# A streaming encoder layer on one core: the chain that prepares x for the second half begins at the eighth group and takes two steps per group from the sixteenth

## The chip, the core and the metric

The kernel runs on one core of a Trainium2 chip. A core has five engines that run side by side, each with its own instruction queue, which it takes in order: PE (matrix products), DVE (vector operations), ACT (copies, casts and activations), POOL (here mostly issues of DMA stores) and SP (issues of DMA loads). Data lies in DRAM, in the on-chip memory, and in eight PSUM banks into which PE writes. Sixteen DMA engines move data, whoever issues the transfer. The metric is the time of one execution on the device in microseconds (us). Lower is better.

## The reference, cut to what matters

One layer, for 2048 prompt tokens and 32 sample tokens, of width 1024, all in float32:

```
h   = RMSNorm(x)
z   = h @ W_in      # columns: q k v | attention gate | B C conv-in conv-gate | merge gates A, B
A   : sliding-window attention with sinks;        yA = (attn * silu(gA)) @ W_A
B   : v = causal conv of width 3 over (C * u);    yB = (B * v * silu(gB)) @ W_B
r   = x + (sigmoid(mA) * yA + sigmoid(mB) * yB) @ W_o
out = r + sigmoid(r @ W_pg) * (p @ W_pp)
```

The change touches only the first two lines: the normed x (h), and the product with W_in.

## The kernel before

**The product h @ W_in.** Tokens come in two halves, the first of 2 x 512 tokens, the second of 2 x 528 with the sample tokens. Columns of W_in come in 21 groups, each a pair of column blocks: groups 0 to 2 "z" (q, k, v), 3 and 4 "ga" (attention gate), 5, 7, 9, 11 "Cu" (C and conv-in), 6, 8, 10, 12 "Bg" (B and conv gate), 13 to 20 "m" (merge gates). For each half and group, a 2 x 2 block product is formed in seven products p = 1 to 7 rather than eight. For this each group needs four sums of its weight quads (`make_sums`, L352 to L368: four loads a, four sums on DVE at L362 to L365, four stores of the sums by POOL at L368), and each half needs sums and differences of blocks of h.

**One product** (`products`, L649 to L654) is four k by three matmuls: a float32 operand is split in two parts, hi by a cast on ACT (L231) and lo = value - hi on DVE (L232), and high x high, high x low and low x high are added in one bank. Weights w are split this way just before use, from a loaded quad (wr) or a sum (a, sc). A step of the list `steps` is a product (half, group, p). In the first half the order within a group is 7, 5, then 6 of the next group, 3, 4, then 1 and 2 of a group two ahead. When product 5 ends, ACT copies the bank a to a tile u (L843, tile u4 of the group) and DVE subtracts the other bank from u later (L848). Product 3 of the same group writes bank a again, so its first matmul waits for that copy. Results go to `consume`: Cu groups are multiplied and run through the three conv taps on DVE (L704 to L726), Bg groups gate them (L735 to L749), m groups end in an activation and a store.

**The chain X1.** The x of the second half is prepared while the first half is multiplied. `second_half` (L582) is a generator of 14 pieces that `next(X1)` runs one at a time: pieces 1 and 2 the norm factors of the first 528 tokens (ten loads of x on SP at L547, ten squares on ACT at L548, a power on POOL at L525; then a diagonal dg on DVE at L530, five transposes a 128 tokens on PE at L532, copies to rb on ACT at L533 and L535), 3 and 4 the same for the other 528, pieces 5 to 8 the row steps k = 0 to 3 (four loads of xT at L594, four norms on DVE at L555, a combine of four operations on DVE at L559 to L562, seven stores xc by POOL at L599), pieces 9 to 14 the quadrants (two loads of xc at L622, a combine of four half-width operations at L559 to L562, four stores xt at L626). After step (0, 20, 2) the kernel takes whatever is left of the chain and reads xc and xt back.

**What sets the order.** `prep` (L1267) is a list of step numbers. After each of these steps one piece of X1 is issued. The tile framework's scheduler then orders every engine's instructions by its own estimate of times, so that the place in `prep` sets roughly where a piece lies, and the neighbours on each engine follow from the scheduler. Loads get their buffers from shared pools (weight quads, and tiles of x and b), so that a load on SP's queue can wait until an earlier tile has been read or stored.

Of the kernel before, what the change touches and what calls it, by code (L numbers as in the profile page):

```python
# [42 lines left out]
def tile_hybrid_stream_step(ctx: ExitStack, tc: tile.TileContext, x, xT, pT, wu, consts, rope, ckT, cv_dup,  # L43
# [201 lines left out]
    G = len(groups)  # L245
# [26 lines left out]
    for gs in sets:  # L272
        g, e = gs[0], gs[-1]
# [624 lines left out]
    def conv_split(b, cs=range(4)):  # L898
        nt = blk(b)[1]
        for c in cs:  # L900
            yc[b, c] = pair(f"ycs{b}_{c}")
            split_half(yc[b, c][0][:, :nt], yc[b, c][1][:, :nt], conv_in.pop((b, c))[:, :nt])
# [342 lines left out]
    at_step = {x: i for i, todo in enumerate(steps) for x in todo}  # L1245
# [18 lines left out]
    conv_at = {(1, G - 2, 1): lambda: conv_load(0), (1, G - 2, 6): lambda: (conv_split(0), conv_load(1)),  # L1264
               (1, G - 1, 6): lambda: conv_split(1), (1, G - 2, 5): lambda: conv_load(2)}
    conv_at.update({(1, sets[-1], 3 + c % 2, "DE"[c // 2]): lambda c=c: conv_split(2, (c,)) for c in range(4)})
    prep = [at_step[0, g, 7] for g in range(5, G)]  # L1267
    for i, todo in enumerate(steps):
        if i < NS:
            continue  # L1270
# [956 lines left out]
```

## Time and profile before

| | |
|---|---|
| median of 3 runs | 1521.99 us (1521.4 to 1523.32) |
| the profiled execution | 1519.46 us |
| its span | 1517.6 us |
| HBM traffic in the span | 246.53 MB read, 130.04 MB written, 248 GB/s |
| PE's clock | 0.998 of full speed, mean |

The span is the time from the first to the last record on the engines. The rows of the profile name an engine, a line, the tile written and the tiles read, a shape and a count. The chain of work that ended last is to 71% PE. The first half of the product with W_in, with the chain X1 beside it, ends near 470 us, and X1 fills roughly 150 to 420 us of it. The same profile by fortieths of the span (37.9 us each), in tenths of busy time:

```profile
PE   9999999989999999999999999999999999999998
DVE  7896778775568887798976978878899999676777
```

### The profile page before, as it was taken

Reading aid. Unit: us, or ns where it says so; the run is one execution under the profiler, and the core shown is the slowest. Engines: PE = TensorE matmul, PEld = TensorE weight load, DVE = VectorE, ACT = ScalarE, POOL = GpSimd, SP = SyncE. Lnnn points to the kernel's source line nnn. Section 1 sums busy time; section 2 is a strip of 40 time slices with the busy share of each in tenths; the row PEclk is TensorE's granted clock in tenths of the full one; section 3 lists DMA queues with packets and bytes.
Section 4 is the critical chain, followed back from the end, with each engine's and each line's share of the span. In section 5 each row is a group of like instructions: output and inputs, shape, how many; then the busy total and the mean of one; then the engine's idle time right before and its main releaser. Section 6 shows DMA issues by size and latency. Waiting matters only on the chain.

```text
span 1517.6 us, 28008 instructions
## 1 busy us (share of the span) xinstructions
PE 1494.1 (98%) x9553; PEld 1350.3 (89%) x9553; DVE 1211.4 (80%) x2310; ACT 801.1 (53%) x1908; POOL 399.0 (26%) x582
## 2 busy tenths in 40 slices
PE   9999999989999999999999999999999999999998
PEld 7878777778889999999999999998888888999998
DVE  7896778775568887798976978878899999676777
ACT  8453442334457655443456645687765686442453
POOL 2133233232201253344333321113232202211201
PEclk9999999999999999999999999999999999999999
DMA  9479987787777897643477975678888958989959
GB/s 357 152 273 346 323 301 276 266 280 246 242 235 241 301 318 246 218 144 123 135 252 263 334 244 185 215 246 242 273 214 271 243 172 246 308 253 273 263 168 286
DMA packets 206670, 378.34 MB, mean 249 GB/s; under 512 B 24896, under 2 KB 58496, under 8 KB 206528
## 3 DMA queue, kind: packets, MB, share of 16 engines
q1 hardware_dynamic: 160608, 258.30, 52.3%
q0 software_dynamic: 36272, 100.44, 22.2%
q10 hardware_dynamic: 9648, 17.83, 3.2%
q8 instruction: 75, 1.23, 0.3%
q14 instruction: 67, 0.55, 0.1%
HBM read 246.53 MB, written 130.04 MB: 248 GB/s over the span
## 4 chain that ended last, share of the span: by engine, by line
PE 71%; DVE 3%; DMA 3%; issue 1%; ACT 1%; POOL 0%; SPq 0%; ACTq 0%; DVEq 0%; POOLq 0%
PE b L160 21%; PE yB L160 6%; PE yA L160 6%; PE a L649 5%; PE a L654 5%; PE a L651 5%; PE la L787 4%; PE O L160 2%; PE c L654 2%; PE c L651 2%; PE c L649 2%; PE lc L787 2%; PE S L160 2%; PE pp L160 2%; PE PT L160 1%
## 5 line engine op out<-in xcount | busy, mean ns | idle before, releaser
L160 PE MATMUL b<-xb_h,w 128*128 128x264 f32 (+1 forms) x1344 | 310.8, 323 | 1.3 <-DVE at L160 1.3
L160 PEld LDWEIGHTS b<-xb_h,w 128*128 128x128 f32 x1344 | 222.6, 188 | 19.5 <-DVE at L160 1.8
L649 PE MATMUL a<-x_h,w 128*128 128x264 f32 (+1 forms) x744 | 229.4, 322 | 7.3 <-ACT u L843 6.9
L651 PE MATMUL a<-x_l,w 128*128 128x264 f32 (+1 forms) x744 | 229.6, 322 | 0.0
L160 PE MATMUL b<-xb_l,w 128*128 128x264 f32 (+1 forms) x672 | 216.5, 322 | 0.0
L654 PE MATMUL a<-x_h,w 128*128 128x264 f32 (+1 forms) x744 | 200.5, 322 | 1.8 <-DVE w L232 1.8
L231 ACT CAST w<-wr 128x512 fp32r<-128x512 f32 (+1 forms) x180 | 110.3, 619 | 97.7 <-PE c L654 39.3
L649 PEld LDWEIGHTS a<-x_h,w 128*128 128x128 f32 x744 | 140.6, 189 | 19.7 <-ACT u L843 7.8
L232 DVE TENSOR_TENSOR w<-wr,w 128x512 fp32r<-128x512 f32 (+1 forms) x180 | 132.9, 747 | 29.3 <-ACT w L231 29.1
L651 PEld LDWEIGHTS a<-x_l,w 128*128 128x128 f32 x744 | 140.6, 189 | 10.6
L654 PEld LDWEIGHTS a<-x_h,w 128*128 128x128 f32 x744 | 124.8, 189 | 13.9 <-DVE w L232 3.0
L160 PEld LDWEIGHTS b<-xb_l,w 128*128 128x128 f32 x672 | 126.4, 188 | 8.6
L160 ACT CAST w<-wr 128x512 fp32r<-128x512 f32 x120 | 73.8, 623 | 97.4 <-PE b L160 50.9
L787 PE MATMUL la<-x_h,w 128*128 128x264 f32 x516 | 111.5, 285 | 2.5 <-DVE s2n L803 1.2
L649 PE MATMUL c<-x_h,w 128*128 128x512 f32 (+1 forms) x336 | 110.9, 340 | 0.7 <-ACT x_h L160 0.7
L651 PE MATMUL c<-x_l,w 128*128 128x512 f32 (+1 forms) x336 | 110.8, 339 | 0.0
L654 PE MATMUL c<-x_h,w 128*128 128x512 f32 (+1 forms) x336 | 100.6, 340 | 0.0
L231 ACT CAST w<-a 128x512 fp32r<-128x512 f32 x82 | 49.6, 620 | 93.7 <-DVE a L364 43.6
L160 DVE TENSOR_TENSOR w<-wr,w 128x512 fp32r<-128x512 f32 x120 | 83.8, 704 | 18.8 <-ACT w L160 18.4
L848 DVE SCALAR_TENSOR_TENSOR u<-u,c 128x264 f32<-128x264 f32 (+1 forms) x125 | 59.5, 506 | 49.2 <-ACT u L843 29.0
L160 PE MATMUL yB<-ycs_h,w 128*128 128x264 f32 (+1 forms) x384 | 91.2, 325 | 0.0
L160 PE MATMUL yA<-ac_h,w 128*128 128x264 f32 (+1 forms) x384 | 90.3, 322 | 0.0
(444 smaller groups left out, 3886.7 us busy)
## 6 DMA issues: line engine op xcount, KB each, us to landing
wr<-in_wu SPq DMA_DIRECT2D x161, 256.0 KB, 4.6
a<-in_wu SPq DMA_DIRECT2D x116, 256.0 KB, 4.7
wr<-ws SPq DMA_DIRECT2D x74, 256.0 KB, 4.2
w<-o SPq DMA_DIRECT2D x32, 512.0 KB, 4.9
ws<-a POOLq DMA_DIRECT2D x63, 256.0 KB, 3.9
w<-wa SPq DMA_DIRECT2D x16, 512.0 KB, 5.3
wr<-qs SPq DMA_DIRECT2D x32, 256.0 KB, 4.1
qs<-a POOLq DMA_DIRECT2D x24, 256.0 KB, 5.7
```

The lines of the kernel that those rows point to most:

```text
L160: return f(**kw)
L231: nc.scalar.copy(out=hi, in_=src)
L232: nc.vector.tensor_tensor(out=lo, in0=src, in1=hi.bitcast(F32), op=sub)
L649: nc.tensor.matmul(out=ps[:, :cn], lhsT=w[:, 0, k], rhs=x[0][:, c0:c0 + cn], start=first and k == 0, stop=False, skip_group_check=True)
L651: nc.tensor.matmul(out=ps[:, :cn], lhsT=w[:, 0, k], rhs=x[1][:, c0:c0 + cn], start=False, stop=False, skip_group_check=True)
L654: nc.tensor.matmul(out=ps[:, :cn], lhsT=w[:, 1, k], rhs=x[0][:, c0:c0 + cn], start=False, stop=k == 3, skip_group_check=True)
L787: nc.tensor.matmul(out=ps[:, :m], lhsT=w[:, a, k], rhs=r[:, cols], start=q in "ABG" and j == 0 and e == 0, stop=j == 1 and e == 2, skip_gr ...
L848: nc.vector.scalar_tensor_tensor(out=t[:, c0:c0 + cn], in0=t[:, c0:c0 + cn], scalar=-1.0, in1=ps[:, :cn], op0=mul, op1=sub)
```

## The change

Before, one piece of the chain is issued after product 7 of each group from 5 on: the norm factors at groups 5 to 8, the row steps at 9 to 12, the quadrants at 13 to 18. After it, pieces begin at group 7, and from group 15 on there is one after product 7 and one after product 3: norm factors at 7 to 10, row steps at 11 to 14, quadrants in twos at 15, 16 and 17.

```diff
-    prep = [at_step[0, g, 7] for g in range(5, G)]
+    prep = [at_step[0, g, p] for g in range(7, G) for p in ((7, 3) if g >= 15 else (7,))]
```

The number of instructions on DVE, ACT, POOL and SP stays the same; their order changes in the part of the program between about 150 and 530 us. Three places follow. In the names, w84 is the 84th weight tile, a12_0 the first quad of group 12 (after L364 it holds a sum), u40_10 the copy u4 of group 10, a0_10_0 the bank a of group 10 and half 0, b00_3 a tile of the row step k = 3.

ACT at the end of group 10, the copy of product 5 and what stands ahead of it. Before:

```order
L231 CAST w81_2686<-wr81_2663 128x512
L231 CAST w82_2703<-sc11_2546 128x512
L231 CAST w83_2738<-a11_1_2540 128x512
L231 CAST w84_2760<-a12_0_2721 128x512
L231 CAST w85_2778<-a11_3_2544 128x512
L843 COPY u40_10_2680<-a0_10_0_2408 128x512
L735 ACTIVATE tg0_2_1_2683<-u40_10_2680 128x512
L843 COPY u20_11_2701<-a0_11_0_2587 128x512
```

After:

```order
L231 CAST w80_2613<-wr80_2581 128x512
L533 COPY rb1_1_2601<-rps1_1_0_2599 128x512
L535 COPY rb1_1_2601<-rps1_1_1_2600 128x16
L843 COPY u40_10_2628<-a0_10_0_2360 128x512
L231 CAST w81_2634<-wr81_2611 128x512
L735 ACTIVATE tg0_2_1_2631<-u40_10_2628 128x512
L843 COPY u20_11_2649<-a0_11_0_2549 128x512
L231 CAST w82_2651<-sc11_2508 128x512
L231 CAST w83_2686<-a11_1_2502 128x512
L231 CAST w84_2708<-a12_0_2669 128x512
L231 CAST w85_2726<-a11_3_2506 128x512
```

The copy u40_10 stood behind the casts of a12_0 (a sum) and a11_3. Now it stands ahead of both, behind the copies to rb of the second norm factor, which have come here.

ACT at the end of group 12. Before:

```order
L231 CAST w97_3095<-a13_1_2895 128x512
L231 CAST w98_3117<-a14_0_3078 128x512
L231 CAST w99_3135<-a13_3_2899 128x512
L843 COPY u40_12_3037<-a0_12_0_2763 128x512
L735 ACTIVATE tg0_3_1_3040<-u40_12_3037 128x512
```

After:

```order
L231 CAST w97_3043<-a13_1_2843 128x512
L843 COPY u40_12_2985<-a0_12_0_2711 128x512
L231 CAST w98_3065<-a14_0_3026 128x512
L231 CAST w99_3083<-a13_3_2847 128x512
L735 ACTIVATE tg0_3_1_2988<-u40_12_2985 128x512
```

The copy u40_12 had three casts ahead in this stretch, among them those of the sum a14_0 and of a13_3. It has moved ahead of these two.

DVE around the sums of group 12 (L362 to L365). Before, with the row step k = 1 (L555, L559 to L562) among them:

```order
L555 SCALAR_TENSOR_TENSOR b10_1_2643<-b10_1_2643,cst_69,rb1_0_1953 128x528
L747 TENSOR_TENSOR cv0_2_0_2576<-s10_10_2421,cv0_2_0_2576 128x512
L555 SCALAR_TENSOR_TENSOR b11_1_2646<-b11_1_2646,cst_69,rb1_1_2298 128x528
L232 TENSOR_TENSOR w83_2738<-a11_1_2540,w83_2738 128x512
L362 TENSOR_TENSOR sc12_2729<-a12_0_2721,a12_1_2723 128x512
L559 TENSOR_TENSOR T3_1_2650<-b11_1_2646,b01_1_2640 128x528
L363 TENSOR_TENSOR a12_1_2723<-a12_1_2723,a12_2_2725 128x512
L560 TENSOR_TENSOR b01_1_2640<-b00_1_2637,b01_1_2640 128x528
L364 TENSOR_TENSOR a12_0_2721<-a12_0_2721,a12_1_2723 128x512
L561 SCALAR_TENSOR_TENSOR T2_1_2649<-b01_1_2640,b11_1_2646 128x528
L365 TENSOR_TENSOR a12_3_2727<-a12_3_2727,a12_0_2721 128x512
```

After, with no row step there:

```order
L232 TENSOR_TENSOR w82_2651<-sc11_2508,w82_2651 128x512
L362 TENSOR_TENSOR sc12_2677<-a12_0_2669,a12_1_2671 128x512
L363 TENSOR_TENSOR a12_1_2671<-a12_1_2671,a12_2_2673 128x512
L364 TENSOR_TENSOR a12_0_2669<-a12_0_2669,a12_1_2671 128x512
L365 TENSOR_TENSOR a12_3_2675<-a12_3_2675,a12_0_2669 128x512
L747 TENSOR_TENSOR cv0_2_1_2542<-a0_10_0_2360,cv0_2_1_2542 128x512
L232 TENSOR_TENSOR w83_2686<-a11_1_2502,w83_2686 128x512
```

The row step k = 1 now stands among the sums of group 14, k = 2 among those of group 15:

```order
L555 SCALAR_TENSOR_TENSOR b10_2_3126<-b10_2_3126,cst_69,rb1_0_2250 128x528
L232 TENSOR_TENSOR w103_3185<-sc14_3034,w103_3185 128x512
L555 SCALAR_TENSOR_TENSOR b11_2_3129<-b11_2_3129,cst_69,rb1_1_2601 128x528
L362 TENSOR_TENSOR sc15_3211<-a15_0_3203,a15_1_3205 128x512
L559 TENSOR_TENSOR T3_2_3133<-b11_2_3129,b01_2_3123 128x528
L363 TENSOR_TENSOR a15_1_3205<-a15_1_3205,a15_2_3207 128x512
L232 TENSOR_TENSOR w104_3220<-a14_1_3028,w104_3220 128x512
L560 TENSOR_TENSOR b01_2_3123<-b00_2_3120,b01_2_3123 128x528
L364 TENSOR_TENSOR a15_0_3203<-a15_0_3203,a15_1_3205 128x512
```

The sum a15_0 (last row) is cast on ACT directly ahead of the copy u40_13:

```order
L231 CAST w103_3185<-sc14_3034 128x512
L231 CAST w104_3220<-a14_1_3028 128x512
L231 CAST w105_3238<-a15_0_3203 128x512
L843 COPY u40_13_3163<-a0_13_0_2890 128x512
L843 COPY u20_14_3183<-a0_14_0_3068 128x512
```

Before, u40_13 stood eight rows ahead of that cast, and quadrant pieces, not a row step, lay beside the sums of group 15.

## The prediction

> **What bounds the kernel now.** I read the page's busy shares first, then the list of waits, then windows, then the timeline at the two longest waits.
>
> ```profile
> PE 1494.1 (98%) x9553; PEld 1350.3 (89%) x9553; DVE 1211.4 (80%) x2310; ACT 801.1 (53%) x1908; POOL 399.0 (26%) x582
> ```
>
> PE is busy 98% of the span. A change that only moves work can win no more than PE's remaining idle time, and a little more where PE runs slowly. So the question is where PE stands in the stretch in which the chain runs. The waits of PE between 160 and 340 us (total, times, longest):
>
> ```profile
> PE a L649 <- ACT u L843: 6.9, 2, 4.4
> PE a L654 <- DVE w L232: 1.1, 1, 1.1
> PE rps L532 <- DVE dg L530: 0.3, 1, 0.3
> PE b L649 <- ACT w L231: 0.2, 1, 0.2
> PE a L649 <- ACT w L231: 0.2, 1, 0.2
> ```
>
> Two waits carry 6.9 of 8.7 us: a product's first matmul (L649, bank a) waits for the copy u (L843) that empties the bank. Two windows show what this costs (columns: length, then PE, weight load, DVE, ACT, POOL busy with counts, granted clock, DMA share, GB/s):
>
> ```profile
> 340.00:440.00 100.00, 100.00 (x433) 81.06 (x432) 57.10 (x92) 43.16 (x77) 19.86 (x37) 1.00 0.76 248
> 160.00:340.00 180.00, 171.40 (x718) 135.17 (x717) 143.87 (x236) 68.43 (x141) 57.45 (x106) 0.98 0.83 284
> ```
>
> From 340 to 440 us PE never stands: 100.00 / 433 = 0.231 us per matmul. Between 160 and 340 us 718 matmuls at that pace would need 165.8 us; 180 were used. **14.2 us** is thus the most that the stretch can give back. The two waits in PE's timeline:
>
> ```profile
> 263.81 0.39 PE L654 MATMUL c<-x_h,w 128*128 128x512 f32 x1
> 266.65 0.50 PE L649 MATMUL a<-x_h,w 128*128 128x512 f32 x1 [2.45 <-ACT u L843]
> ...
> 271.06 0.43 PE L649 MATMUL c<-x_h,w 128*128 128x512 f32 x1
> ```
>
> ```profile
> 307.69 0.40 PE L654 MATMUL c<-x_h,w 128*128 128x512 f32 x1
> 312.53 0.80 PE L649 MATMUL a<-x_h,w 128*128 128x512 f32 x1 [4.44 <-ACT u L843]
> ...
> 316.77 0.40 PE L649 MATMUL c<-x_h,w 128*128 128x512 f32 x1
> ```
>
> A product is 12 matmuls (four k, three each at L649, L651, L654), so from the first row to the last of each fence 13 matmuls start: 13 x 0.231 = 3.00 us. Stall A takes 271.06 - 263.81 - 3.00 = **4.25 us**, stall B 316.77 - 307.69 - 3.00 = **6.08 us**. Both are longer than the waits in them (2.45, 4.44), because PE runs slowly behind the wait:
>
> ```profile
> 266.65:271.06 4.41, 4.41 (x12) 3.46 (x13) 2.54 (x5) 1.10 (x2) 1.07 (x2) 0.62 0.99 316
> ```
>
> Twelve matmuls took 4.41 us, not 2.77, at a granted clock of 0.62. [...]
>
> Why the copy is late shows on ACT and DVE before stall B (the first two rows are ACT's):
>
> ```profile
> 310.85 1.14 ACT L231 CAST w<-a 128x512 fp32r<-128x512 f32 x2 [7.69 <-DVE a L364]
> 311.90 0.58 ACT L843 COPY u<-a 128x512 f32<-128x512 f32 x1
> ```
>
> ```profile
> 301.33 0.77 DVE L555 SCALAR_TENSOR_TENSOR b<-b,cst,rb 128x528 f32<-128x528 f32 x1 [0.34 <-DMA b<-in_xT]
> ...
> 305.08 1.44 DVE L555 SCALAR_TENSOR_TENSOR b<-b,cst,rb 128x528 f32<-128x528 f32 x2
> ...
> 308.24 0.70 DVE L559 TENSOR_TENSOR T<-b,b 128x528 f32<-128x528 f32 x1
> ...
> 310.08 0.68 DVE L364 TENSOR_TENSOR a<-a,a 128x512 f32<-128x512 f32 x1
> ```
>
> ACT takes its queue in order. It stood 7.69 us at two casts for a sum of DVE (L364), with the copy behind them. The sum was late because row step k = 3 of the chain (norms L555, combine L559 to L562) stood among the conv taps and sums in DVE's queue. Stall A is the same with k = 1.
>
> **The change, part by part.** It adds and removes no instruction of DVE, ACT, POOL or SP. The chain's 14 pieces move later: the two norm factors to groups 7 to 10, row steps to 11 to 14, quadrants to 15 to 17, two in each.
>
> Stalls A and B. In ACT's changed order the copy of group 10 stands ahead of the casts of the sums of group 12, with no row step in DVE's queue before those sums; the copy of group 12 has one cast (of group 13's sum, made a group earlier) ahead, and the cast of a sum of group 14 has gone behind it. A cast costs 0.57 us of ACT's queue (1.14 for two) where nothing is late. Both stalls go: -4.25 - 6.08 = -10.33 us. What is late next is priced below.
>
> The third loss is where the second norm factor's x loads lie before the weight loads on SP:
>
> ```profile
> 206.00:218.00 12.00, 10.77 (x46) 7.71 (x46) 10.09 (x18) 6.53 (x15) 6.08 (x10) 1.00 0.91 313
> ```
>
> ```profile
> 206.28 0.69 DVE L362 TENSOR_TENSOR sc<-a,a 128x512 f32<-128x512 f32 x1 [5.01 <-DMA a<-in_wu]
> ```
>
> DVE stood 5.01 us for a weight load, and PE lost 12 - 10.77 = 1.23 us afterwards. In the changed order that factor's loads come two groups later, without the quad loads beside them; but the first factor's loads now come at this place, ahead of the same weights. Nothing to 1.23 us goes; I take half, -0.6 us.
>
> Row steps. Four times four norms and a combine; they cost DVE the same wherever they lie:
>
> ```profile
> L555 DVE SCALAR_TENSOR_TENSOR b<-b,cst,rb 128x528 f32<-128x528 f32 x16 | 11.9, 761 | 0.7 <-DMA b<-in_xT 0.7
> L559 DVE TENSOR_TENSOR T<-b,b 128x528 f32<-128x528 f32 x4 | 2.8, 701 | 0.0
> ```
>
> Per step 4 x 0.76 + 4 x 0.70 = 5.8 us. The places given up were a Cu and a Bg group twice. The new ones are Cu, Bg, m, m; DVE is 80% busy from 160 to 340 us (143.87 of 180) but 57% from 340 to 440, where only m groups run. So the steps k = 2 and 3 go where DVE has spare time, and k = 1 goes to group 12, where k = 3 made stall B. There DVE is as full as before, and only ACT's order saves it.
>
> The new tight place is group 13, where ACT's copy u stands right behind a cast of group 15's sum, the pattern of stalls A and B with one cast. That sum stands on DVE behind k = 2's four norms, whose loads wait for buffers that k = 1's stores must have read. Landing times from 160 to 340 us (KB each, median us):
>
> ```profile
> b<-in_xT SPq DMA_DIRECT2D x16, 264.0 KB, 4.8
> ...
> xc<-T POOLq DMA_DIRECT2D x12, 264.0 KB, 4.1
> ...
> xt<-in_x SPq DMA_DIRECT2D x9, 256.0 KB, 6.0
> xq<-xc SPq DMA_DIRECT2D x4, 264.0 KB, 4.8
> xt<-xq POOLq DMA_DIRECT2D x7, 132.0 KB, 3.1
> ```
>
> From k = 1's T at L561 to the copy: about 4.1 for the store, 4.8 for a load and some 3 for issues and for the later loads' spacing (my estimate: three loads of 264 KB at 284 GB/s are 2.9 us), then a norm and six rows of DVE to the sum (7 x 0.62 by start-to-start distances such as 310.08 - 308.24 over three rows), 0.57 and 0.58 on ACT: 17.4 us. A group is seven products, 84 x 0.231 = 19.4 us of PE. About two us are left, and less where L561 comes late in its group: I take 1 to 2, so no wait. Bounds of this term: 0, and stall B's 6.08.
>
> Quadrants, two per group. A piece moves 2 x 264 + 4 x 132 KB = 1.08 MB, and one more per group of 19.4 us adds 56 GB/s. At 248 GB/s for a share of 0.76 that is 0.17 more of the DMA engines, 0.93 together. On DVE it is four operations of half width in a stretch with 43% idle: nothing. I take no cost, with a bound of 3 x 1.23 us (the loss at share 0.91 above, in each of three groups). [...] No row of the run before has two pieces in one group.
>
> **Sum:** -10.33 - 0.6 = -10.9 us. The profiled execution of 1519.46 us (span 1517.6) would become 1508.5. The median of the runs is 1521.99, 2.5 above it; the same difference gives 1521.99 - 10.9 = **1511.1 us**.
>
> **Rivals.**
> (1) A stall moves rather than goes: group 13's copy (or group 12's, with k = 1) waits as in A or B. For: order and engines are the same pattern, with one or two us to spare. Against: one cast, not two, and no taps beside k = 2. It returns 4.25 to 6.08: **1515.4 to 1517.2**.
> (2) The doubled quadrants delay weight loads: +3.7, **1514.8**. For: 0.91 with 1.23 us lost. Against: the 4.41 us behind stall A, at a share of 0.99, hold no other wait, and a row step's four loads and seven stores of 264 KB (3.0 MB in a group) are more than two pieces.
> (3) No change: both places stall again, groups 12 and 13: 1511.1 + 10.33 = **1521.4**. The change would do what it says, and its gain be absorbed.
> (4) Slower: each row step's loads follow the stores of the step before through the shared buffers. If landing takes 6.0 us, as the x loads did, rather than 4.1 and 4.8, the chain of 17.4 grows by 3.1 to 20.5, over a group's 19.4, and DVE stands before the sums in each of groups 11 to 14. Four stalls of A's or B's size cost 17.0 to 24.3: **1528 to 1535**. It decides from three such stalls on: 10.9 + 3.0 = 13.9 us must be lost. Against: only 0.7 us of all sixteen norms' time was waiting for loads.
>
> **How the numbers follow.** Forecast 0.52, (1) 0.23, (2) 0.07, (3) 0.11, (4) 0.07. A measurement of this kernel can tell about 0.2%, 3 us, from no change. Faster by more: forecast, (1), (2), 0.82; within: 0.11; slower: 0.07. The range: all of the 14.2 gone is 1507.8, and another 1.2 of this row, whose order also moves, 1506.6:
>
> ```profile
> L787 PE MATMUL la<-x_h,w 128*128 128x264 f32 x516 | 111.5, 285 | 2.5 <-DVE s2n L803 1.2
> ```
>
> Above, (1) with the third loss unchanged is 1517.8, with another wait of 1.2 us 1519. So 1506.5 to 1519 holds the first three cases, 0.82.
>
> **What would show it.** Right: no wait of PE for ACT's u between 160 and 340 us, no stretch at a clock near 0.6, the whole stretch some 11 us shorter, and everything behind it as before. Wrong: such a wait at group 13, near 317 us, with ACT standing for L364 (1); waits of L649 or L654 for w from 340 to 400 us with a share over 0.9 (2); DVE idle for b<-in_xT before the norms (4).

## The result and the profile after

The changed kernel takes **1504.74 us** (median of 4 runs, 1503.43 to 1506.17) where the kernel before took 1522.28 us in the same comparison (1521.4 to 1523.32, 4 runs): a ratio of 0.9885 with a 95% interval of 0.9868 to 0.9902, 17.5 us less. The forecast was 1511.1 us with a range from 1506.5: the sign was right, and the time is 1.8 us below the range. The profiled execution took 1504.31 us, its span is 1502.5 us, 15.1 us less than before.

The busy shares on the page of the changed kernel:

```profile
PE 1488.1 (99%) x9553; PEld 1350.1 (90%) x9553; DVE 1209.8 (81%) x2310; ACT 801.4 (53%) x1908; POOL 398.1 (26%) x582
```

The two windows of before, now of the changed kernel (same columns):

```profile
160.00:340.00 180.00, 180.00 (x781) 145.42 (x780) 146.76 (x239) 72.83 (x148) 55.83 (x103) 1.00 0.82 286
340.00:440.00 100.00, 100.00 (x439) 81.30 (x438) 61.71 (x109) 46.28 (x82) 21.48 (x40) 1.00 0.83 278
```

PE does not stand once in 280 us. 781 matmuls now fit where 718 did, at a clock of 1.00. In the first window DVE is busy 146.76 us, against 143.87 before. The list of PE's waits has no row left between 160 and 340 us.

The place that the prediction called tight, group 13, in the timelines of DVE (first row), ACT (two rows) and PE (last two):

```profile
316.71 0.69 DVE L364 TENSOR_TENSOR a<-a,a 128x512 f32<-128x512 f32 x1
```

```profile
317.49 0.62 ACT L231 CAST w<-a 128x512 fp32r<-128x512 f32 x1 [3.42 <-DVE a L364]
318.01 1.07 ACT L843 COPY u<-a 128x512 f32<-128x512 f32 x2
```

```profile
318.60 0.39 PE L654 MATMUL c<-x_h,w 128*128 128x512 f32 x1
318.83 0.39 PE L649 MATMUL a<-x_h,w 128*128 128x512 f32 x1
```

The pattern of the stalls is there: ACT stands 3.42 us for the sum, with the copy behind it. But the first of the two copies is done about half of 1.07 us after 318.01, and product 3 starts at 318.83, on time. The margin is some 0.3 us, less than the 1 to 2 us that the prediction gave it. In the second profile of the changed kernel (e5 below) nothing of it is left: the copies begin at 318.14, and product 3 starts 0.30 us behind the matmul before it, 0.07 us late.

```profile
318.47 0.39 PE L654 MATMUL c<-x_h,w 128*128 128x512 f32 x1
318.77 0.50 PE L649 MATMUL a<-x_h,w 128*128 128x512 f32 x1
```

**Where the time came from.** The undisturbed distance from one matmul's start to the next is 0.2325 us here. The table adds up what longer distances (over 0.29 us) have above that, between 140 and 445 us of each profile, by place: near the norm factors (178 to 235 us; in the changed kernel 208 and 246 us, where their transposes now lie), stall A (group 10), stall B (group 12), and anything else.

| kernel | norm factors | A | B | other | sum |
|---|---|---|---|---|---|
| before | 2.78 | 4.23 | 6.06 | 1.00 | 14.1 |
| after | 0.21 | 0 | 0 | 0 | 0.2 |

So 13.9 of the 15.1 us of span come from this stretch. The rest is spread over the beginning and the part behind 445 us.

### The profile page after: what moved, and what is told of

Read it like the earlier page. It is cut to its first block, busy times and chain, and to the rows that moved or that the text cites. A ratio compares the mean times of both kernels' runs of the same rounds, so it can differ in the third digit from the quotient of the medians.

```text
span 1502.5 us, 27997 instructions
## 1 busy us (share of the span) xinstructions
PE 1488.1 (99%) x9553; PEld 1350.1 (90%) x9553; DVE 1209.8 (81%) x2310; ACT 801.4 (53%) x1908; POOL 398.1 (26%) x582
## 3 DMA queue, kind: packets, MB, share of 16 engines
q8 instruction: 75, 1.23, 0.3%
## 4 chain that ended last, share of the span: by engine, by line
PE 94%; DVE 2%; DMA 1%; ACT 1%; issue 1%; POOL 0%; DVEq 0%; ACTq 0%; POOLq 0%; SPq 0%
PE b L160 21%; PE a L654 7%; PE a L649 7%; PE a L651 7%; PE yB L160 6%; PE yA L160 6%; PE la L787 5%; PE c L654 4%; PE c L651 4%; PE c L649 4%; PE pp L160 3%; PE lc L787 2%; PE O L160 2%; PE S L160 2%; PE PT L160 1%; PE lb L787 1%
## 5 line engine op out<-in xcount | busy, mean ns | idle before, releaser
L649 PE MATMUL a<-x_h,w 128*128 128x264 f32 (+1 forms) x744 | 227.8, 320 | 0.2 <-ACT w L231 0.2
L649 PEld LDWEIGHTS a<-x_h,w 128*128 128x128 f32 x744 | 139.9, 188 | 11.0 <-ACT w L231 0.4
L649 PE MATMUL c<-x_h,w 128*128 128x512 f32 (+1 forms) x336 | 110.6, 340 | 0.7 <-ACT x_h L160 0.7
L848 DVE SCALAR_TENSOR_TENSOR u<-u,c 128x264 f32<-128x264 f32 (+1 forms) x125 | 59.6, 508 | 37.6 <-ACT u L843 22.3
```

The source lines that it names most:

```text
L649: nc.tensor.matmul(out=ps[:, :cn], lhsT=w[:, 0, k], rhs=x[0][:, c0:c0 + cn], start=first and k == 0, stop=False, skip_group_check=True)
L848: nc.vector.scalar_tensor_tensor(out=t[:, c0:c0 + cn], in0=t[:, c0:c0 + cn], scalar=-1.0, in1=ps[:, :cn], op0=mul, op1=sub)
```

## The experiments

Theory 1: the whole gain is what PE lost in that stretch, and stalls A and B are copies of a bank that stand on ACT behind casts of sums, which DVE makes late because a row step stands among them. The rivals are with each run. The second run is the changed kernel; the others differ from before in `prep` alone, save the two under "ACT's order". "Lost" is the sum of the table above for that kernel's profile.

**The two kernels again.**

> The kernel before, unchanged, for a second profile. Theory 1 (the whole gain is what PE loses between 160 and 340 us, and that loss differs from execution to execution, because landing times set how late the sums are): time 1521 to 1524 us, PE waits for ACT's u at groups 10 and 12 again, but together at another size than 6.9 us, by 1 us or more, and the profiled time follows it. Rival (part of the gain lies outside that stretch, and the stretch always loses the same): the two waits within 0.5 us of 2.4 and 4.4, and any difference of the profiled time lies behind 340 us.

1520.51 us (11 runs), beside 1520.33 us for the same kernel in 21 runs: nothing differs, as it should be. The second profile has the same two waits, 7.1 us together instead of 6.9. So in these two profiles the waits do not differ by a microsecond, and that half of theory 1 falls. What differs is what follows them. PE at stall A in this profile:

```profile
263.12 0.39 PE L654 MATMUL c<-x_h,w 128*128 128x512 f32 x1
265.96 0.50 PE L649 MATMUL a<-x_h,w 128*128 128x512 f32 x1 [2.45 <-ACT u L843]
266.30 0.40 PE L651 MATMUL a<-x_l,w 128*128 128x512 f32 x1
...
268.85 0.40 PE L649 MATMUL c<-x_h,w 128*128 128x512 f32 x1
```

The wait is 2.45 us as in the first profile, but the twelve matmuls behind it take 2.89 us (265.96 to 268.85) instead of 4.41: behind a first distance of 0.34 us they start 0.23 to 0.24 us apart, where in the first profile eight distances of 0.39 to 0.43 us follow, and stall A cost 2.7 us, not 4.2. Behind stall B (4.60 us here) the slow stretch was longer (twelve distances of 0.42 to 0.43 us, 311.05 to 316.17, where the first profile has five), 7.45 us lost in all. The stretch lost 13.2 us, against 14.1.

> The changed kernel once more, timed beside the kernel before on one chip in more rounds. Theory 1 (the whole gain is what PE lost between 160 and 340 us, 14.2 us, and about one us of small waits behind it, as the two profiles have it): 14.5 to 16 us faster than the kernel before in the same runs. Rival (the 17.5 us between the first medians is real, and the profiled execution of the kernel before was a favourable one): 17 to 18 us faster.

1504.29 us against 1520.53 us (10 runs), ratio 0.9894 (0.9879 to 0.9908): 16.2 us. This lies between the two expectations. The changed kernel took the same time in both comparisons (1504.74, 1504.29), and it was the kernel before that stood at 1522.28 in the first and at 1520.3 to 1520.5 in all later ones. The spans of the second pair of profiles differ by 15.0 us, of which 12.8 lie between 140 and 445 us.

**The two parts of the change.**

```diff
-    prep = [at_step[0, g, 7] for g in range(5, G)]
+    prep = [at_step[0, g, 7] for g in range(7, G)]
```

> Begins with group 7 as the change, but one piece per group throughout, so that the last two pieces run where the chain's results are read back. Theory 1 (only the place of the norm factors and row steps counts): 1503 to 1507 us, no wait of PE for ACT's u. Rival (taking quadrants in twos brings a part): 1507 to 1512 us, with new waits of PE at the end of the first half, near 440 to 480 us, where the two pieces are run together with the first loads back.

1505.13 us, ratio 0.9901 (0.9888 to 0.9915), lost 0.2. Starting with group 7 alone brings the gain.

```diff
-    prep = [at_step[0, g, 7] for g in range(5, G)]
+    prep = [at_step[0, g, p] for g in range(5, G) for p in ((7, 3) if g >= 15 else (7,))]
```

> Begins with group 5 as before, with two pieces per group from group 15. Theory 1: 1520 to 1524 us, both waits for ACT's u as before. Rival (the earlier end of the chain brings a part): 1515 to 1519 us with the same two waits.

1521.14 us, ratio 1.0003 (0.9994 to 1.0013), lost 13.8, with both waits (7.0 us together). Taking quadrants in twos brings and costs nothing.

**The terms one at a time.**

```diff
-    prep = [at_step[0, g, 7] for g in range(5, G)]
+    prep = [at_step[0, g, p] for g in (5, 6, 7, 8, *range(11, G)) for p in ((7, 3) if g >= 15 else (7,))]
```

> Norm factors at groups 5 to 8 as before, row steps and quadrants where the change has them. Theory 1 with its terms: both waits for ACT's u are gone, the losses near 178 and 206 to 218 us beside the norm factors stay (2 to 4 us): 1506 to 1510 us. Rival (the early x loads of the norm factors hold back the weight loads so that everything behind runs late, and they are the main cause): 1512 us or more, with a wait for u left.

1507.1 us, ratio 0.9911 (0.9897 to 0.9924), lost 1.9, all beside the norm factors. This is 2.8 us more than the changed kernel's 1504.29, of which the stretch shows 1.7 (1.9 less 0.2): the norm factors' place is worth more than the 0.6 us that the prediction gave it.

```diff
-    prep = [at_step[0, g, 7] for g in range(5, G)]
+    prep = [at_step[0, g, p] for g, p in [(5, 7), (6, 7), (7, 7), (8, 7), (9, 7), (11, 7), (11, 3)] + [(g, 7) for g in range(12, 19)]]
```

> As before, but row step k = 1 goes from group 10 to group 11 (product 7) and k = 2 follows there at product 3; k = 3 stays at group 12. In ACT's order the copy of group 10 then stands ahead of the casts of a sum that a row step delays; the copy of group 12 stays behind the casts of a14_0 and a13_3. Theory 1: stall A gone, stall B left: one wait for ACT's u, at group 12, 3 to 6 us; 4 to 5 us faster than before. Rival (a row step beside the conv taps costs PE the same wherever it lies in these groups): as before within 2 us, or a wait at group 11.

1516.49 us against 1520.53, ratio 0.9972 (0.9961 to 0.9983): 4.0 us. The row for u in the list of waits between 140 and 345 us:

```profile
PE a L649 <- ACT u L843: 5.0, 1, 5.0
```

Stall A is gone, stall B is left and a little longer (lost 7.5 us there).

```diff
-    prep = [at_step[0, g, 7] for g in range(5, G)]
+    prep = [at_step[0, g, p] for g, p in [(g, 7) for g in (5, 6, 7, 8, 9, 10, 11, 13, 14, 15, 16, 17, 18, 19)]]
```

> As before, but row step k = 3 goes from group 12 to group 13 and the quadrants follow one group later. In ACT's order the copy of group 12 then stands ahead of the casts of a14_0 and a13_3. Theory 1: stall B gone, stall A left: one wait for ACT's u of 2 to 3 us at group 10; 5.5 to 7 us faster than before. Rival (the stall follows the row step): a wait for u at group 13, less than 3 us faster.

1512.92 us, ratio 0.9953 (0.9936 to 0.9969): 7.6 us, a little above the expectation. The same row:

```profile
PE a L649 <- ACT u L843: 2.5, 1, 2.5
```

Stall B is gone and A is left, at 4.2 us. So each stall goes with its own row step, by about its size in the first profile.

```diff
-    prep = [at_step[0, g, 7] for g in range(5, G)]
+    prep = [at_step[0, g, p] for g in range(6, G) for p in ((7, 3) if g >= 15 else (7,))]
```

> Begins with group 6, in twos from group 15: row steps at groups 10 to 13. In ACT's order the copy of group 10 stands ahead of the cast of the sum a12_0, the copy of group 12 behind those of a14_0 and a13_3, as before. Theory 1 (the order of copy and cast decides): one wait for u, at group 12, 2 to 5 us, and 1508 to 1513 us where before is 1520 to 1522. Rival (a later start alone helps, by freeing the DMA engines early on, whatever the order on ACT): no wait for u and 1504 to 1507 us; second rival (a row step in a Bg group stalls whatever the order): waits at 10 and 12, 1515 us or more.

1513.13 us, ratio 0.995 (0.9935 to 0.9965), lost 6.3: one stall at group 12, and nothing beside the norm factors, which stood at groups 6 to 9.

```profile
303.95 0.50 PE L649 MATMUL a<-x_h,w 128*128 128x512 f32 x1 [4.26 <-ACT u L843]
```

One group earlier than the change, and more than half of the gain is missing. Time and wait are those of theory 1; the rival by which a later start helps whatever the order on ACT falls.

**ACT's order.** The chain stays as before, but the casts of a12_0, a11_3, a14_0 and a13_3 are queued behind the copies u4 of groups 10 and 12 (their instructions are kept in u4_of as they are issued). The edit moves later lines by three to five: L652 is the former L649, L846 L843, L853 L848, and L563 to L565 are L560 to L562.

```diff
-            split(w[:, 0, :n], w[:, 1, :n], raw_of.pop(i)[:, :n])
+            behind = worder[i][0] == "s" and worder[i][1] == 0 and u4_of.get({6: worder[i][2] - 2, 3: worder[i][2] - 1}.get(worder[i][3]))
+            with tc.issue_after(behind) if behind else nullcontext():
+                split(w[:, 0, :n], w[:, 1, :n], raw_of.pop(i)[:, :n])
...
+                if name == "u4" and h == 0 and g in (10, 12):
+                    u4_of[g] = inst.ins if hasattr(inst, "ins") else inst
```

> The chain as before (from group 5, one piece per group), but on ACT the casts of the sum a12_0 and of a14_0 (and of a11_3, a13_3) are queued behind the copies of groups 10 and 12 respectively; the row steps stay among DVE's sums. Theory 1 (the place of the copy behind a cast makes the stalls, and the late sum alone costs PE nothing): both waits for ACT's u gone, about 10 us faster than before, 1509 to 1512 us; what stays is the loss beside the norm factors. Rival (the row steps in DVE's queue are the cost, and PE then waits for the late weights instead): waits of L649 or L654 for w of 2 us or more at the same places, less than 6 us faster.

1515.57 us against 1520.41, ratio 0.9964 (0.9952 to 0.9975): 4.8 us, half of what theory 1 gave. ACT now makes the two copies at 258.44 and 300.77 us, in time. Stall A shrank to 0.65 us, stall B only to 4.1 us, and at both PE waits for something else. PE, then DVE, at stall B in this kernel's timelines:

```profile
309.42 0.80 PE L652 MATMUL c<-x_h,w 128*128 128x512 f32 x1 [2.44 <-DVE u L853]
```

```profile
305.50 0.69 DVE L364 TENSOR_TENSOR a<-a,a 128x512 f32<-128x512 f32 x1
306.10 0.70 DVE L563 TENSOR_TENSOR b<-b,b 128x528 f32<-128x528 f32 x1
306.72 0.69 DVE L365 TENSOR_TENSOR a<-a,a 128x512 f32<-128x512 f32 x1
307.32 0.70 DVE L564 SCALAR_TENSOR_TENSOR T<-b,b 128x528 f32<-128x528 f32 x1
308.06 0.71 DVE L565 SCALAR_TENSOR_TENSOR T<-T,b 128x528 f32<-128x528 f32 x1
308.69 0.68 DVE L853 SCALAR_TENSOR_TENSOR u<-u,c 128x512 f32<-128x512 f32 x1
```

With the copy on time, the next product (p = 4, bank c) waits for DVE, which empties bank c by u - c (the former L848) behind the last of the row step. Theory 1 saw one of two ways in which the row step holds PE. The rival named DVE rightly, and its time came true, but the wait is for a bank and not for weights. The first way shows at a new place too: at 284.37 us, in group 11, whose copy was left where it stood, PE waits 0.74 us for a copy behind a cast that stood 4.50 us for a sum, and 1.0 us is lost there. This run varies more than ACT's order, for the scheduler moved rows of DVE as well: the first norm of k = 3 stands 4.9 us ahead of product 3 (299.09 to 304.02), where it stood 6.6 us ahead of product 3's place before (worked out below).

With the same order on ACT and the start at group 6:

```diff
-    prep = [at_step[0, g, 7] for g in range(5, G)]
+    prep = [at_step[0, g, p] for g in range(6, G) for p in ((7, 3) if g >= 15 else (7,))]
```

> Begins with group 6, in twos from group 15, and ACT's copies of groups 10 and 12 ahead of the casts as in the run with the chain as before. If the terms add up (stall at group 12 removed by the order of ACT alone; the norm factors lose nothing at groups 6 to 9): 1503.5 to 1506 us, as the changed kernel, with no wait of PE between 160 and 340 us. If the later start itself is needed: 1508 us or more.

1510.7 us, ratio 0.9932 (0.9917 to 0.9947), lost 4.6: again a wait for DVE's u at group 12 (2.87 us) and a slow stretch behind it. The terms do not add up to the changed kernel by ACT's order; the row step itself has to stand elsewhere or earlier.

**Why k = 1 does no harm in group 12.** In the changed kernel a row step stands in the very group of stall B. The first norm there and where PE went on, in DVE's and PE's timeline of the changed kernel:

```profile
287.87 0.76 DVE L555 SCALAR_TENSOR_TENSOR b<-b,cst,rb 128x528 f32<-128x528 f32 x1
...
300.15 0.68 DVE L848 SCALAR_TENSOR_TENSOR u<-u,c 128x512 f32<-128x512 f32 x1
```

Product 3 of group 12 began at 299.30 us and product 4 at 302.11, by PE's timeline. The first norm came 11.4 us ahead of product 3, and DVE emptied bank c (300.15 to 300.83) 1.3 us before it was needed. Before, the first norm came at 301.33, 6.6 us ahead of where product 3 should have begun (307.69 + 0.23); in e8 it was 4.9 us (294.61 against 299.52), as in e9. Bank a is saved by ACT's order, as the prediction said:

```profile
294.46 0.58 ACT L843 COPY u<-a 128x512 f32<-128x512 f32 x1
299.12 1.14 ACT L231 CAST w<-a 128x512 fp32r<-128x512 f32 x2 [4.09 <-DVE a L364]
```

Behind these two casts, where it stood in the kernel before, the copy would have been done near 300.7 us (my estimate from their times), 1.4 us after product 3 began. So the new place works by two things: the copy stands ahead of the casts, and DVE is through the step in time for bank c. The kind of group alone does not decide. No run varies one of the two alone.

**Later still.**

```diff
-    prep = [at_step[0, g, 7] for g in range(5, G)]
+    prep = [at_step[0, g, p] for g in range(9, G) for p in ((7, 3) if g >= 15 else (7,))]
```

> Begins with group 9, in twos from group 15: norm factors at 9 to 12, all row steps in m groups (13, 14, and two at 15), quadrants at 16 to 18. Theory 1 (between 160 and 440 us PE has nothing more to win): 1503.5 to 1506.5 us. Rival (the two row steps in group 15 fill DVE and the DMA engines, and the chain's end comes closer to where its results are read): a new wait of PE from 350 us on, 1507 to 1515 us.

1504.73 us, ratio 0.9897 (0.9882 to 0.9912), lost 0.2. The window where its last two row steps and all quadrants lie (the first two row steps run from 302.7 to 330 us):

```profile
340.00:440.00 100.00, 100.00 (x437) 81.06 (x436) 71.30 (x124) 45.68 (x81) 29.04 (x54) 1.00 0.94 329
```

A share of 0.94 of the DMA engines over 100 us cost PE nothing here (busy 100.00 of 100.00 us, 437 matmuls). No version was found that beats the changed kernel.

```diff
-    prep = [at_step[0, g, 7] for g in range(5, G)]
+    prep = [at_step[0, g, p] for g, p in [(g, 7) for g in range(10, 14)] + [(g, p) for g in range(14, 19) for p in (7, 3)]]
```

> The chain as late as it fits: norm factors at 10 to 13, then two pieces per group at 14 to 18, so row steps at 14 and 15 in twos and quadrants at 16 to 18. In ACT's order the copy of group 15 stands behind the cast of the sum a17_0, the pattern of the stalls. Theory 1 with timing deciding: between 1504 us (sum in time) and 1511 us (one stall of up to 6 us at group 15). Rival (m groups have spare time on DVE, so no stall can come there): 1506.5 us at most and no wait for u.

1511.55 us, ratio 0.9946 (0.9929 to 0.9962). Half a microsecond above the expectation. The waits from 340 us on:

```profile
PE a L654 <- DVE w L232: 2.5, 1, 2.5
PE a L649 <- ACT u L843: 1.2, 1, 1.2
PE c L649 <- DVE u L848: 0.8, 1, 0.8
```

The three waits lie from 357 to 376 us, in m groups, and cost 7.4 us there. The rival (no stall can come in m groups) falls. Two row steps listed for one group are not the cause by themselves: e11 has two at group 15 and loses nothing. Its last two row steps begin 20 us apart (341.15, 361.21), those of e12 12 to 15 us (340.88, 353.57, 368.55). That this spacing decides is my reading; no run varies it alone.

**The norm factors.** What was open after this: which factor loses what PE lost near 178 and 210 to 217 us.

```diff
-    prep = [at_step[0, g, 7] for g in range(5, G)]
+    prep = [at_step[0, g, p] for g, p in [(5, 7), (6, 7), (8, 7), (9, 7)] + [(g, 7) for g in range(11, 15)] + [(g, p) for g in range(15, 18) for p in (7, 3)]]
```

> Norm factors: the first at groups 5 and 6 as before, the second at 8 and 9; row steps at 11 to 14 and quadrants in twos from 15, as the change has them. Theory (what PE loses at 210 to 217 us comes from the second factor's ten x loads, which stand on SP ahead of group 9's weight loads): that loss (2.1 us) gone, the 0.5 us near 178 us left, 1504.5 to 1506 us. Rival (any norm factor before group 9 costs PE 1 to 2 us): a loss of 1 us or more near 225 us, 1506 us or more.

1505.36 us, ratio 0.9902 (0.9885 to 0.9918), lost 2.0: the 0.54 us near 178 us stays, the loss at 210 to 217 us is gone, and 1.34 us are lost at 229 to 231 us, where PE waits 1.1 us for a copy on ACT (s, L843). The time fits the theory, and the loss near 229 us fits the rival.

```diff
-    prep = [at_step[0, g, 7] for g in range(5, G)]
+    prep = [at_step[0, g, p] for g, p in [(6, 7), (6, 3), (7, 7), (8, 7)] + [(g, 7) for g in range(11, 15)] + [(g, p) for g in range(15, 18) for p in (7, 3)]]
```

> Norm factors: the first at group 6 (both pieces), the second at 7 and 8; the rest as the change has it. The second factor's x loads stand ahead of three of group 9's four weight loads, close behind the first factor's. Theory (x loads ahead of group 9's weights make the loss at 210 to 217 us): DVE waits for a<-in_wu again near 205 us and PE loses 1 to 2.5 us behind it, 1505.5 to 1507.5 us. Rival (only the first factor at group 5 made SP late): no loss there, 1503.5 to 1505 us.

1510.24 us, ratio 0.9933 (0.9919 to 0.9948), lost 7.5. Both expectations miss: PE waits 3.7 us, but at group 6. PE, then ACT, in this profile:

```profile
177.74 0.40 PE L654 MATMUL a<-x_h,w 128*128 128x512 f32 x1
181.83 0.79 PE L649 MATMUL a<-x_h,w 128*128 128x512 f32 x1 [3.69 <-ACT u L843]
```

```profile
179.10 0.62 ACT L548 ACTIVATE xt<-xt 128x512 f32<-128x512 f32 x1
179.63 0.19 ACT L548 ACTIVATION_READ_ACCUMULATOR xt<-xt 128x1 f32 x1
180.58 0.63 ACT L548 ACTIVATE xt<-xt 128x512 f32<-128x512 f32 x1 [0.76 <-DMA xt<-in_x]
181.12 0.19 ACT L548 ACTIVATION_READ_ACCUMULATOR xt<-xt 128x1 f32 x1
181.21 0.56 ACT L843 COPY u<-a 128x512 f32<-128x512 f32 x1
```

It is the stall of A and B with another operation in front: the copy that empties bank a stands behind squares (L548) whose x loads land late. At 210 to 217 us nothing is lost, in e13 or in e14: the second factor at groups 7 and 8 makes that loss only in the runs in which the first stands at 5 and 6.

## Why the prediction was wrong

**Stalls A and B: right in place and size.** The prediction took 10.33 us for both. The first profile lost 4.23 + 6.06 us there, the second 2.71 + 7.45, the changed kernel nothing, and each goes alone with its row step (runs e6 and e7). That the slow clock adds to a wait was right as well, but the addition is not fixed: behind the same wait of 2.45 us it was 1.6 us in one profile and 0.1 us in the other.

**The mechanism: right for the copies on ACT, incomplete.** Putting the copies first, with the chain as before, brought half (e9). The row step also delays DVE's own emptying of bank c.

**The third loss: the term that failed.** The prediction took half of 1.23 us, PE's idle time in one window, as -0.6 us. PE lost 2.78 us beside the norm factors (0.54 near 178 us, 0.1 near 195, 2.13 from 210 to 217), and all but 0.2 went: the term should have been -2.6 us. Two readings were wrong: idle time leaves out distances that are longer without a gap in PE's busy time, and halving it had no row behind it. Leaving the norm factors at the old place costs 2.8 us (e4). Why they cost PE at groups 5 to 8 and not at 6 to 9 or 7 to 10 is only partly settled: the idle time of DVE before group 9's sums (5.01 us) is gone in the changed kernel, but e13 and e14 show losses at other places instead. The order on SP alone was not tried.

**The rest of the 14.2 us.** The prediction knew that the stretch could give back 14.2 us, and counted only the named parts, 10.9. Another 1.0 us (0.44 near 238 us and 0.56 near 296) went too. Both are gone in every kernel in which row step k = 1 no longer stands at group 10, but the first is missing in the second profile of before and in e3 as well, so no cause is shown for it.

**The base: the step that put the range too high.** The sum was carried from the profiled execution (1519.46 us) to the median of three runs (1521.99) as a fixed offset of 2.5 us. The kernel before has medians of 1520.3 to 1520.5 us in the later comparisons (7 to 21 runs), and the profiled execution lay within their spread, 1518.8 to 1523. In the changed kernel the median lies 0.4 us above the profiled execution (1504.74, 1504.31), not 2.5. The range's lower end stood too high for the same reason: 15.4 us of gain were allowed, but from the higher base. From 1520.4 us the same 15.4 reach 1505.0, so the base explains 1.6 of the 1.8 us by which the time fell below the range.

**The sum of the misses.** The forecast was 6.4 us too high, and four terms account for 6.3. The offset makes 2.1 (2.5 less 0.4), the third loss 2.0 (2.6 less 0.6), the losses near 238 and 296 us 1.0, and 1.2 lie outside the stretch (15.1 less 13.9), with no cause shown. A and B were read from the same profile that gives 4.23 and 6.06, so that each size is met to 0.1 us proves little; the second profile of before splits them as 2.7 and 7.45, and only their sum holds (10.3 and 10.2).

**The rivals.** (1) did not happen, but by 0.3 us or less at group 13, where 1 to 2 us were claimed. The chain priced at 17.4 us took 20.1, from the end of k = 1's L561 (298.41) to the end of the copy (318.55). Its loads came as priced: the norms of k = 2 begin at 310.35, 11.9 us after L561. But from the first norm to the sum lie eleven rows of DVE and 7.1 us, not seven rows and 4.3. It came out in time because L561 stands 1.6 us ahead of product 3 of its group, which the prediction had not worked out: that part was luck. e8 and e12 show stalls with the chain one group earlier or its row steps closer together, at 6 to 7 us. (2) did not happen: e3 shows no effect of the doubling, and e11 none of a share of 0.94. (3) did not happen. Of (4) the sign came and the cost did not: DVE stood 4.8 us for b<-in_xT before norms (2.2 us in e5) where it stood 0.7 before, and PE never waited for it.

**Still open.** One to two microseconds of the gain (15 to 16 us in most comparisons) lie outside the 12.8 to 13.9 us that the stretch shows. Set matmul against matmul in PE's order, the two pairs of profiles gain 0.3 and 0.6 us before 140 us, where no piece of the chain has been issued yet, and 0.2 and 1.2 us between 445 and 520 us. No run tells these from the scatter of single executions.

## What to carry to other kernels

Look at what stands in its queue in front of the instruction that empties a PSUM bank. In the kernel before, ACT stood idle for 7.69 us at two casts, up to 310.85 us, and began the copy behind them at 311.90, though the copy's product had started its last matmul at 304.90. Where the work in front waited for a sum or a load that came late, PE waited too: 2.45 and 4.44 us behind casts of sums (before) and 3.69 us behind squares of late x (e14). Here moving the late work by two groups brought 15 to 16 us and reordering the queue 4.8, because the same work delays the other bank through its own engine as well (2.44 us of PE's waiting in e9); and the new place is right only if the work is done before the product that follows, so read the margin from the timeline (here 0.3 us in one execution and none in another) and not from the kind of work around it. When a stretch of the critical engine has a known total loss, forecast from that total and say which part stays, rather than adding up the waits that have a name, and start from the median of many runs rather than from one execution and an offset.

## What the runs showed of the hardware

The clock behind a wait was not fixed by its length. A gap of 2.83 to 2.84 us from start to start was followed by distances of 0.42 to 0.43 us between matmuls in three profiles (before, e7, e9) and, behind a first one of 0.34, by distances of 0.23 to 0.24 us in one (the second profile of before). In the kernel before, the granted clock was 0.50 over seven distances of 0.42 to 0.43 us (268.07 to 271.06) and 1.00 from 340 to 440 us, at 0.231 us per matmul. After the longer gaps, 3.25 us in e10, 4.09 in e14, 4.66 in e8, 4.84 in before and 5.44 in e6, and after stall B in the second profile of before (a wait of 4.60 us), the distances went to 0.43 us every time, for 5 to 12 matmuls, which cost 1.4 to 2.7 us beyond the gap. Why the same gap had two outcomes no run shows.
